# Hybrid decoder block on one core: second turns behind two columns, nine more small products, the first unit's tail in a hand-written order, and the second half's operands tied to the units

## The chip, the cores and the metric

One core of a Trainium2 chip runs the whole block in one launch. The metric is device time in microseconds (us), the median of several runs. TensorE (PE) multiplies, VectorE (DVE), ScalarE (ACT) and GpSimd (POOL) do the elementwise work, and SyncE (SP) issues all DMAs. Each engine works through its own queue in order.

## What is computed

The input is x, 2048 positions by 1024 features, in float32. The part that the change touches is the first third:

```
h    = rmsnorm(x, norm1_g)
proj = h @ w_in                      # 1024 x 3088
p_q, p_k, p_v, p_g, p_a, c_b, c_c, c_h = split(proj)
log_a  = log_sigmoid(p_a @ w_gate_up + b_gate) / 16
o_gla  = rmsnorm(gla_chunked(q, k, v, log_a)) * silu(p_g)
o_conv = c_b * conv3(c_c * c_h)
x = x + concat(o_gla, o_conv) @ w_out
x = x + (silu(h2 @ w_gate) * (h2 @ w_up)) @ w_down     # h2 = rmsnorm(x, norm2_g)
return rmsnorm(x, norm_f_g)
```

## The kernel before

**Number format.** Every large product is made of three passes: a float32 operand is split into a high part (`hi`, rounded on ACT) and a low part (`lo`, the difference, on DVE), and PE adds hi*hi, hi*lo and lo*hi (lines 412 to 414 and 686 to 688, each a 128x128 weight against 512 positions).

**Seven-product units.** Positions go in two halves of 1024, each of two blocks of 512. `unit` multiplies a 2x2 grid of weight quarters with a 2x2 grid of operand quarters in seven products instead of eight. The operands are B11, T1, T2, B21, T3, B22, T4, the weights A11, S1, S2, A12, S3, S4, A22, in that order. `unit_weights` loads the four raw quarters, makes S1 to S4 from them with four subtractions and additions (`mix`, line 384 or 386) and splits all seven (`weight_quarter`). One product is 12 matmuls. The products accumulate in PSUM; after products 4, 5 and 6 (indices 3, 4, 5) DVE adds a product to a kept tile (`plus`, line 443), and ACT copies others out (`copied`, line 450). Index 6 goes on in the bank that index 4 left (`oa`), so it must wait until `plus(c22, oa)` has read it.

**The opening.** For the first half the kernel begins with plain products, so that PE can start before the operands of the units exist. `opening` turns the rows of x with PE transposes (`turned(0)`: features 0 to 511, `turned(1)`: 512 to 1023, line 598), splits the turned tiles (`taken`), and adds up columns k = 0 to 7 for two rows of the weights (`column`). Twelve small products of a tile of ones precede it (`warm`, line 709). The squares for the norm (`square`, line 612) and the estimate of the norm's factor (`estimate`, `spread`) run on ACT and DVE beside it, and `turn` spreads the factor over the partitions with four PE transposes (line 652). Then come the columns of the second weight unit, the operands of the units (`normed`, `final`, `made`), the gate's small product (line 890), and the first unit, on `win[2]`.

**Order.** A planner places the instructions of each engine when the program is built, by their place in the program, by what is ready, and by its own estimates of durations. While the list `ordered` holds something, ACT's and DVE's instructions of the opening are chained by hand instead (`queued`), and a low part is issued only after the next high part (`late`, `catch_up`). `behind(marks)` puts instructions behind marked ones on the same engine, without a semaphore. The first unit's weights and its last operands, T3 and T4, are made in this chain; then `ordered` is cleared, and the unit's `plus` stand behind the chain's last low part (`given`).

**Background.** `tick` is called after every product and advances a list of generators by one step: at every tick while `hurry` holds, else at every second one. First come the gate's decays (`gate`, `forget_gate`) in turn with the squares of blocks 2 and 3 (`row_stats`), then `unhurried`, then `h1_ahead`, which makes the second half's operands: `combine` loads 16 tiles of x (`quad`), scales each on DVE (`scaled`, line 814), takes differences on POOL (lines 327 to 340), splits four of the seven kinds, and stores them. `gla_half` follows it. After the ten units of the first half (`in_proj(0)`: `win[2]`, then 3 to 11; 6 to 8 and 9 to 11 are the convolution's, with lines 966, 972 and 979 on DVE) the rest of `h1_ahead` is drained, and `load_pairs` loads the operands back.

## Time and profile before

| | |
|---|---|
| median of 3 runs | 2065.07 us (2064.35 to 2069.71) |
| the profiled execution, its own time | 2064.27 us |
| its span | 2062.5 us |
| mean granted TensorE clock over the span | 0.996 |
| busy, PE / DVE / ACT / POOL | 2024.1 / 1430.6 / 961.0 / 848.4 us |

The span runs from the first to the last recorded instruction; the run's own time is 1.8 us longer. In the views, L12 is line 12 of the kernel, "out<-in" names the tiles written and read, and the brackets at the end of a line of the timeline hold the idle time before that instruction and what ended it. A window's line gives the busy time of PE, PE's weight loads, DVE, ACT and POOL, then the granted clock as a share of full speed, the DMA engines' busy share and GB/s.

### The profile page before, as it was taken

The page shows a single profiled execution, that of the slowest core. Times are in us where ns is not written, and L with a number is a line of the kernel's source. Part 1 is how long each engine was busy: PE and PEld are TensorE (multiplying, and loading weights), DVE is VectorE, ACT ScalarE, POOL GpSimd, SP SyncE. Part 2 cuts the span into 40 slices and gives each one's busy share as a digit, 9 for nine tenths or more (in the row PEclk, how much of TensorE's full clock was granted, in tenths as well). Part 3 has the DMA queues.
Part 4 walks back from the last instruction along what each step waited for, and adds up shares of the span by engine and source line. Part 5 has one row for each costly group of instructions (what it writes and reads, how often), then busy time and mean ns, then how long its engine had stood idle before and what let it go on. Part 6 is the DMA issues. An engine that isn't in the chain of part 4 may idle for free.

```text
span 2062.5 us, 27137 instructions
## 1 busy us (share of the span) xinstructions
PE 2024.1 (98%) x9253; PEld 1660.3 (81%) x9253; DVE 1430.6 (69%) x2140; ACT 961.0 (47%) x1922; POOL 848.4 (41%) x618
## 2 busy tenths in 40 slices
PE   9999999999999999999999999999999999999997
PEld 7777888887888888888888888787888888888786
DVE  7888676559743786677676577776766666677774
ACT  5664455666543344444444452334434444453344
POOL 0136322222102474464464345533644554444544
PEclk9999999999999999999999999999999999999999
DMA  7378495425686873555444576476444444486653
GB/s 255 102 241 301 137 345 151 148 82 168 206 282 226 332 277 123 181 194 193 171 175 164 211 275 250 182 285 273 153 179 163 159 158 168 172 312 223 237 214 127
DMA packets 189738, 422.54 MB, mean 205 GB/s; under 512 B 19904, under 2 KB 65184, under 8 KB 180128
## 3 DMA queue, kind: packets, MB, share of 16 engines
q1 hardware_dynamic: 189600, 420.81, 57.6%
q8 instruction: 73, 1.20, 0.2%
q14 instruction: 65, 0.53, 0.1%
HBM read 276.02 MB, written 144.70 MB: 204 GB/s over the span
## 4 chain that ended last, share of the span: by engine, by line
PE 86%; DVE 7%; DMA 2%; ACT 2%; issue 1%; POOL 1%; SPq 0%; DVEq 0%; ACTq 0%; POOLq 0%
PE mm L412 24%; PE mm L414 24%; PE mm L413 24%; PE mm L1131 3%; PE mm L1132 3%; PE mm L1134 3%; DVE wq L192 2%; DMA op<-shT 1%; PE a_ps L890 1%; PE mm L688 1%; PE mm L686 1%; PE mm L687 1%; PE o_ps L1055 1%; PE o_ps L1057 1%; DVE op L192 1%
## 5 line engine op out<-in xcount | busy, mean ns | idle before, releaser
L412 PE MATMUL mm<-op,wq 128*128 128x512 f32 x2467 | 962.6, 393 | 14.9 <-ACT c L450 6.8
L413 PE MATMUL mm<-op,wq 128*128 128x512 f32 x2467 | 960.4, 390 | 0.3 <-DVE op L192 0.2
L414 PE MATMUL mm<-op,wq 128*128 128x512 f32 x2467 | 949.6, 390 | 4.3 <-DVE wq L192 4.2
L192 DVE TENSOR_TENSOR wq<-raw,wq 128x512 fp32r<-128x512 f32 (+2 forms) x612 | 495.3, 814 | 255.0 <-ACT wq L191 252.5
L191 ACT ACTIVATE wq<-raw 128x512 fp32r<-128x512 f32 (+2 forms) x612 | 355.6, 587 | 575.8 <-PE mm L414 441.3
L412 PEld LDWEIGHTS mm<-op,wq 128*128 128x128 f32 x2467 | 463.3, 188 | 120.0 <-ACT c L450 10.4
L414 PEld LDWEIGHTS mm<-op,wq 128*128 128x128 f32 x2467 | 463.3, 188 | 105.5 <-DVE wq L192 8.5
L413 PEld LDWEIGHTS mm<-op,wq 128*128 128x128 f32 x2467 | 463.7, 188 | 95.6 <-DVE op L192 1.8
L386 POOL TENSOR_TENSOR raw<-s,raw 128x512 f32<-128x512 f32 (+2 forms) x96 | 124.1, 1293 | 503.5 <-DVE wq L192 465.3
L386 POOL TENSOR_TENSOR raw<-raw 128x512 f32<-128x512 f32 (+2 forms) x192 | 255.0, 1334 | 123.6 <-DVE wq L192 118.9
L386 POOL TENSOR_TENSOR s<-raw 128x512 f32<-128x512 f32 (+2 forms) x96 | 126.4, 1317 | 290.5 <-DMA raw<-in_wffn_dram 83.6
L443 DVE TENSOR_TENSOR c<-mm,c 128x512 f32<-128x512 f32 x198 | 135.6, 686 | 69.0 <-PE mm L414 67.0
L443 DVE TENSOR_TENSOR y<-mm,y 128x512 f32<-128x512 f32 x185 | 126.9, 687 | 81.5 <-PE mm L414 80.9
L1113 POOL TENSOR_TENSOR ssx<-ssx,q 128x512 f32<-128x512 f32 x52 | 77.3, 1501 | 160.6 <-ACT q L1112 160.3
L450 ACT ACTIVATE c<-mm 128x512 f32<-128x512 f32 x198 | 115.6, 586 | 15.1 <-PE mm L414 12.9
L1131 PE MATMUL mm<-op,wq 128*128 128x512 f32 x256 | 100.9, 395 | 0.0
L1132 PE MATMUL mm<-op,wq 128*128 128x512 f32 x256 | 99.7, 390 | 0.0
L191 ACT ACTIVATE wq<-s 128x512 fp32r<-128x512 f32 (+2 forms) x96 | 56.1, 585 | 86.7 <-PE mm L414 83.8
L192 DVE TENSOR_TENSOR wq<-s,wq 128x512 fp32r<-128x512 f32 (+2 forms) x96 | 85.3, 888 | 2.8 <-ACT wq L191 2.1
L1134 PE MATMUL mm<-op,wq 128*128 128x512 f32 x256 | 79.7, 390 | 0.0
L192 DVE TENSOR_TENSOR op<-op 128x512 fp32r<-128x512 f32 x94 | 76.5, 841 | 4.3 <-ACT op L191 4.3
L1326 POOL TENSOR_TENSOR y<-x,y 128x512 f32<-128x512 f32 x32 | 53.7, 1678 | 44.7 <-DVE y L443 40.4
(222 smaller groups left out, 1845.9 us busy)
## 6 DMA issues: line engine op xcount, KB each, us to landing
raw<-in_wffn_dram SPq DMA_DIRECT2D x44, 1024.0 KB, 6.4
sa_B<-so SPq DMA_DIRECT2D x47, 512.0 KB, 4.3
op<-sa_B SPq DMA_DIRECT2D x47, 512.0 KB, 6.8
raw<-in_win_dram SPq DMA_DIRECT2D x22, 1024.0 KB, 5.9
sa_T<-so SPq DMA_DIRECT2D x44, 512.0 KB, 4.5
op<-sa_T SPq DMA_DIRECT2D x44, 512.0 KB, 6.6
raw<-in_wdown_dram SPq DMA_DIRECT2D x24, 768.0 KB, 5.5
sx<-y SPq DMA_DIRECT2D x48, 256.0 KB, 3.9
```

Of the source, the lines that this page charges most:

```text
L191: last_hi[:] = [act.activation(hi, src, AF.Copy)]
L192: last_lo[:] = [dve.tensor_tensor(lo, src, hi.bitcast(F32), ALU.subtract)]
L386: pool.tensor_tensor(*args)
L412: pe.matmul(o[:], wh, xh, start=first and k == 0, stop=False, skip_group_check=True)
L413: pe.matmul(o[:], wh, xl, start=False, stop=False, skip_group_check=True)
L414: return pe.matmul(o[:], wl, xh, start=False, stop=k == n - 1, skip_group_check=True)
L443: dve.tensor_tensor(t[:], o[:], t[:], ALU.add)
L450: last_out[:] = [act.activation(t[:], o[:], AF.Copy)]
L1113: pool.tensor_tensor(ssq[:], ssq[:], q[:], ALU.add)
L1131: pe.matmul(o[e, j][:], wh, m[:, 0, :], start=k == 0, stop=False)
L1132: pe.matmul(o[e, j][:], wh, m[:, 1, :], start=False, stop=False)
L1134: pe.matmul(o[e, j][:], wl, ops[k][j][:, 0, :], start=False, stop=k == KD - 1)
```

## The change

1. In `opening`, nine small products of ones follow `turned(0)`, and `turned(1)` is placed behind two columns (k = 0, 1) instead of three; column 2 moves behind it.
2. The first unit's tail stays in the hand-written chain. `T4` is no longer made before the unit's products but in a generator `rest`: tiles 0 and 1 ahead of `plus(c11, ...)`, tile 2 ahead of `plus(c22, ...)`, tile 3 behind it, then the split of A22; only then is `ordered` cleared, and `held` keeps the chain's last high and low part. The first two `plus` are links of the chain; the third stands behind `held`. The first five ticks return without a step of the background, and `row_stats` and the gate's copies stand behind `held`.
3. The second unit's mixing (`win[3]`) goes from POOL to DVE.
4. `h1_ahead` becomes `h1_paced`: each scaling stands behind the latest `plus` on DVE, and from `unhurried` on every fourth tick makes two steps until `h1_paced` ends.

```diff
 def tick():
     pace[0] += 1
+    if ordered:
+        return
     if pace[0] % 2 == 0 or hurry:
         step()
+        if steady and pace[0] % 4 == 0:
+            step()
...
 def unhurried():
     hurry.clear()
+    steady.append(True)
     yield
+
+def h1_paced():
+    with_marks.append(True)
+    yield from h1_ahead()
+    with_marks.clear()
+    steady.clear()
...
         def quad():
...
-            return scaled(col(g + k), rb[j], h)
+            with behind(last_plus if with_marks else []):
+                return scaled(col(g + k), rb[j], h)
...
         def mix(*args):
...
-                pool.tensor_tensor(*args)
+                eng.tensor_tensor(*args)
...
-        w["A22"] = weight_quarter(a22)
-        others()
+        w["A22"] = a22 if ordered else weight_quarter(a22)
...
-        given = []
-        if ordered:
-            catch_up()
-            ordered.clear()
-            given += last_lo
...
 def plus(t, o):
-    with behind(given):
-        dve.tensor_tensor(t[:], o[:], t[:], ALU.add)
+    if ordered:
+        queued(dve, lambda: dve.tensor_tensor(t[:], o[:], t[:], ALU.add))
+    else:
+        with behind(held if rest is not None else []):
+            last_plus[:] = [dve.tensor_tensor(t[:], o[:], t[:], ALU.add)]
     return t
...
-        plus(c11, mul(3))
+        o = mul(3)
+        then()
+        plus(c11, o)
         mul(4, oa)
+        then()
         plus(c22, oa)
+        if rest is not None:
+            next(rest, None)
+            w["A22"] = weight_quarter(w["A22"])
+            held[:] = last_hi + last_lo
+            ordered.clear()
         mul(5, ob)
...
-            with behind(last_out or unit_splits):
+            with behind(last_out + held):
...
         for j in range(2):
             stack = bx[0].tile([96, PB], F32R, name="a_sb", tag="b")
...
-            with behind(after):
+            with behind(held):
...
         turned(0)
+        for _ in range(9):
+            pe.matmul(warm[:, 0:P], ones[:], ones[:], start=True, stop=True)
...
-        for k in range(3):
+        for k in range(2):
             for r in range(2):
                 mark = column(0, 0, r, k)
         with behind([mark]):
             turned(1)
...
-        for k in range(3, 6):
+        for k in range(2, 6):
...
+        def rest():
+            difference("T4", 0)
+            difference("T4", 1)
+            yield
+            difference("T4", 2)
+            yield
+            difference("T4", 3)
+            h.clear()
...
-                yield unit(win[u], ops)
+                yield unit(win[u], ops, eng=dve if (half, u) == (0, 3) else pool)
```

More of the change, by code (lines that the diff above doesn't have):

```diff
@@ L801, in opening @@
         catch_up()
-        after = []
-        steps = gate(0, ops, mark, after)
+        steps = gate(0, ops, mark)
         next(steps)
@@ L806, in opening @@
         between = [
-            [lambda: out(1, 1, 0)], [lambda: out(1, 1, 1)], [partial(made, "T3"), lambda: after.extend(last_hi)], [],
-            [partial(made, "T4")],
-        ]
-        return ops, raw2, between, steps
+            [lambda: out(1, 1, 0)], [lambda: out(1, 1, 1)], [partial(made, "T3")],
+        ]
+        def rest():
[6 more added lines that the diff above has]
+            h.clear()
+        return ops, raw2, between, steps, rest()
     def scaled(g, rb, h, into=None):
@@ L876, in second_factor, with gate @@
         dve.memset(carry[:], 0.0)
-    def gate(half, ops, mark=None, after=()):
+    def gate(half, ops, mark=None):
         a = bank("a_ps")
@@ L939, in forget_gate, with in_proj @@
         store(s_d[b][i][:], t2[:])
-    def in_proj(half, ops, raw=None, between=()):
+    def in_proj(half, ops, raw=None, between=(), rest=None):
         def units():
             if half == 0:
-                yield unit(win[2], ops, raw=raw, between=between)
+                yield unit(win[2], ops, raw=raw, between=between, rest=rest)
             for u in range(0 if half else 3, 12):
-                yield unit(win[u], ops)
+                yield unit(win[u], ops, eng=dve if (half, u) == (0, 3) else pool)
         units = units()
@@ L1436, in tile_hymba_block @@
     act.preload_act_table_set("natural_log_exp_and_others")
-    ops, raw, between, steps = opening()
+    ops, raw, between, steps, rest = opening()
     hurry.append(True)
@@ L1440, in tile_hymba_block @@
         [
-            in_turn(steps, row_stats(2), row_stats(3)), unhurried(), h1_ahead(),
+            in_turn(steps, row_stats(2), row_stats(3)), unhurried(), h1_paced(),
         ]
     )
-    in_proj(0, ops, raw, between)
+    in_proj(0, ops, raw, between, rest)
     drain_background(lambda: len(background) < 2)
```

13 lines of the change are left out of this document (8 added, 5 removed).

## The prediction, made before the changed kernel was run

> **What bounds the kernel now.** I read the head of the page, then the chain that ended last, then PE's busy time by windows.
>
> ```profile
> span 2062.5 us, 27137 instructions
> PE 2024.1 (98%) x9253; PEld 1660.3 (81%) x9253; DVE 1430.6 (69%) x2140; ACT 961.0 (47%) x1922; POOL 848.4 (41%) x618
> ...
> PE 86%; DVE 7%; DMA 2%; ACT 2%; issue 1%; POOL 1%; SPq 0%; DVEq 0%; ACTq 0%; POOLq 0%
> ```
>
> PE is the bound: 86% of the last chain, and only 2062.5 - 2024.1 = 38.4 us of the span without a matmul. A change of order can win back idle time and time at a lower clock, nothing else. So the question is how much of both lies where the change reaches, the first 230 us.
>
> ```profile
> 60.00:92.00 32.00, 28.65 (x119) 23.01 (x118) 28.06 (x42) 18.63 (x39) 4.52 (x3) 0.95 0.24 73
> 92.00:132.00 40.00, 38.39 (x167) 30.41 (x166) 37.15 (x87) 30.54 (x71) 10.93 (x8) 1.00 0.69 230
> 132.00:176.00 44.00, 44.00 (x198) 36.44 (x197) 32.06 (x40) 22.06 (x38) 26.58 (x18) 1.00 0.83 283
> 176.00:216.00 40.00, 35.13 (x147) 26.65 (x146) 37.82 (x49) 19.32 (x41) 22.26 (x15) 1.00 0.77 247
> 216.00:256.00 40.00, 39.95 (x177) 32.76 (x176) 24.25 (x33) 15.24 (x31) 13.98 (x10) 1.00 0.35 124
> ```
>
> The second number of a row is PE's busy time. It falls short by 3.35 us in the stretch of the first unit, by 1.61 in the next, by nothing from 132 to 176, by 4.87 from 176 to 216, where DVE is busy 37.82 of 40 us, and by nothing again after that. The opening, before 60, is the fourth place.
>
> **Step 1, the opening.** PE's timeline, then ACT's and DVE's:
>
> ```profile
> 1.12 4.88 PE L709 MATMUL warm<-ones 128*128 128x128 f32 x24 [1.12 <-DVE ones L79]
> 5.84 2.49 PE L598 MATMUL xt<-ident,xr 128*128 128x128 f32 x16
> 10.33 0.51 PE L686 MATMUL mm<-op,wq 128*128 128x512 f32 x1 [2.00 <-ACT op L178]
> ...
> 16.73 1.91 PE L598 MATMUL xt<-ident,xr 128*128 128x128 f32 x16
> 18.40 0.48 PE L686 MATMUL mm<-op,wq 128*128 128x512 f32 x1
> ...
> 23.86 0.64 PE L652 MATMUL rb_ps<-ident,rep 128*128 128x128 f32 x4 [1.12 <-DVE rep L642]
> ```
> ```profile
> 15.15 0.19 ACT L612 ACTIVATION_READ_ACCUMULATOR q<-xr 128x1 f32 x1
> 18.35 0.69 ACT L178 ACTIVATE op<-xt,sml 128x512 fp32r<-128x512 f32 x1 [3.02 <-PE xt L598]
> ```
> ```profile
> 11.84 0.75 DVE L185 SCALAR_TENSOR_TENSOR op<-xt,sml,op 128x512 fp32r<-128x512 f32 x1
> 13.00 0.75 DVE L185 SCALAR_TENSOR_TENSOR op<-xt,sml,op 128x512 fp32r<-128x512 f32 x1 [0.41 <-ACT op L178]
> ```
> ```profile
> 13.00:14.00 1.00, 1.00 (x4) 0.71 (x4) 0.75 (x1) 1.00 (x3) 0.00 (x0) 0.50 1.09 422
> 16.00:17.00 1.00, 1.00 (x7) 0.78 (x6) 0.00 (x0) 0.00 (x0) 0.00 (x0) 1.00 1.04 406
> ```
>
> After the first turns (end 8.33) PE is idle for 2.00 us, and soon after that the granted clock is 0.50: 18 matmuls of three columns take 10.33 to 16.73. Behind them the second turns begin, and ACT, done with all else at 15.34, sits 3.02 us until they end. From there ACT and DVE lead the chain to the factor, for which PE waits 1.12 us at 23.86.
>
> The nine small products are 18 records (the twelve show as 24). I take 0.12 us each, as the turns of 16.73 have (1.91 / 16): 2.2 us, about the idle time; they end near 10.5, and the window in front of the columns is busy, so I take the clock as staying full. Two columns, 12 matmuls, then end with the low part of x's second tile (11.84 + 0.75 = 12.59) and two matmuls of 0.23 more: 13.1. The turns take 18.40 - 16.73 = 1.67 and end at 14.8, before ACT is free at 15.34. So ACT's chain moves by 18.35 - 15.34 = 3.0 us and no further, and the factor with it. Column 2, which now follows the turns, brings PE to 14.8 + 24 x 0.228 = 20.3, still ahead of the factor at 20.9. **Term: -3.0 us.** Bounds: if the clock falls as before, 12 matmuls last until 15.3, the turns until 17.0, and 1.4 us are won; if the small products run at the 0.203 us of the first twelve (4.88 / 24), they end at 12.0, 1.7 us late, and with a low clock behind them 0.3 us are lost. I take the upper end, because each cause is removed at its place; what is late next is ACT itself, whose order is unchanged.
>
> The Trainium skill, "TensorE: Matmul & The Clock Gate", Part 1, says that the gate watches windows of some 3.4 us which run free of the kernel's start. By that rule an idle time of 2 us lowers the clock in one execution and not in another. No second profile of this kernel is here to show it; what it would mean is the fourth rival.
>
> **Step 2, the first unit.** PE, its clock, and what DVE does meanwhile:
>
> ```profile
> 67.64 0.40 PE L412 MATMUL mm<-op,wq 128*128 128x512 f32 x1
> ...
> 83.83 0.39 PE L414 MATMUL mm<-op,wq 128*128 128x512 f32 x1
> 87.57 0.76 PE L412 MATMUL mm<-op,wq 128*128 128x512 f32 x1 [3.35 <-DVE c L443]
> ...
> 90.63 0.39 PE L413 MATMUL mm<-op,wq 128*128 128x512 f32 x1
> ```
> ```profile
> 88.00:89.00 1.00, 1.00 (x4) 0.71 (x4) 0.94 (x3) 0.00 (x0) 0.00 (x0) 0.50 0.63 205
> ```
> ```profile
> 64.01 0.69 DVE L384 TENSOR_TENSOR s<-raw 128x512 f32<-128x512 f32 x1
> ...
> 66.86 3.53 DVE L182 TENSOR_TENSOR wq<-raw,wq 128x512 fp32r<-128x512 f32 x2
> ...
> 75.74 1.29 DVE L182 TENSOR_TENSOR op<-h,op 128x512 fp32r<-128x512 f32 x2 [1.49 <-ACT op L178]
> ...
> 78.27 0.68 DVE L907 TENSOR_TENSOR a_sb<-a_ps,a_sb 32x512 fp32r<-32x512 f32 x1
> ...
> 85.42 0.69 DVE L182 TENSOR_TENSOR wq<-raw,wq 128x512 fp32r<-128x512 f32 x1
> 86.14 1.89 DVE L443 TENSOR_TENSOR c<-mm,c 128x512 f32<-128x512 f32 x3
> ```
> ```profile
> 66.84 1.30 POOL L386 TENSOR_TENSOR s<-raw 128x512 f32<-128x512 f32 x1 [65.03 <-DVE wq L182]
> ```
>
> Six products, 72 matmuls, run from 67.64 to 84.06: 0.228 us a matmul. The seventh waits until 87.57 for the second of three `plus`, which all stand behind the last low part of the chain, A22's at 85.42. That costs 3.51 us, and the restart at half clock (7 matmuls in 90.63 - 87.57 = 3.06 us instead of 1.60) costs 1.46 more: 4.97 together.
>
> DVE's work in front of that point holds three things that the change takes out. Two splits take 3.53 us where two others take 1.29 (75.74): 2.24 us beside POOL's first mixing at 66.84, which goes to DVE (three of 0.69, as at 64.01, later or in gaps). The gate's two differences, 1.36 us, go behind `held`. 1.49 us of waiting for ACT fall where ACT squares rows; these now come after the fifth tick. So A22's low part could end near 86.1 - 5.1 = 81.0, and with two `plus` (0.63 each) ahead of it, at 82.3.
>
> In the new order, c11's `plus` needs the end of product index 3 (78.6) and c22's that of index 4 (67.64 + 60 x 0.228 = 81.3). Behind the latter stand T4's last difference, two low parts and A22's, with `plus` five items of 0.60 to 0.63: 81.4 + 3.1 = 84.5. The seventh product's first two matmuls (from 84.06) need none of these low parts of A22, the third starts at 84.5. So a wait of 0 to 0.3 us is left, and no lower clock. **Term: -4.7 us.** Bounds: 0 if DVE still ends at 86, -5.0 if nothing waits.
>
> What is late next is the second unit. DVE then has, in a row, the third `plus` 0.6, A11's low part 0.6, three mixings 2.1, the gate's two differences 1.4 and S1's low part 0.6: 5.3 us from 84.5, so 89.8, where product index 1 needs S1's low part at 86.8 + 2.73 + 0.46 = 90.0. The gate's decays also move up against it, in the row 92:132 where DVE has only 2.85 us free. **Term: +1.0 us** (0 to +3). The delayed background costs PE nothing else: the five lost steps are made good by the doubled ones.
>
> **Step 3, the second half's operands.**
>
> ```profile
> 126.67 0.74 DVE L814 SCALAR_TENSOR_TENSOR h<-h,sml,rb_ps 128x512 f32<-128x512 f32 x1
> ...
> 192.35 0.74 DVE L814 SCALAR_TENSOR_TENSOR h<-h,sml,rb_ps 128x512 f32<-128x512 f32 x1
> 193.01 0.68 DVE L443 TENSOR_TENSOR c<-mm,c 128x512 f32<-128x512 f32 x1
> 193.61 1.77 DVE L192 TENSOR_TENSOR wq<-s,wq 128x512 fp32r<-128x512 f32 x1
> ```
> ```profile
> L814 DVE SCALAR_TENSOR_TENSOR h<-h,sml,rb_ps 128x512 f32<-128x512 f32 x6 | 4.4, 739 | 3.1 <-DMA h<-in_xt_dram 3.1
> ```
> ```profile
> 182.24 0.50 PE L412 MATMUL mm<-op,wq 128*128 128x512 f32 x1 [1.14 <-ACT c L450]
> ...
> 203.00 0.50 PE L414 MATMUL mm<-op,wq 128*128 128x512 f32 x1 [0.99 <-DVE wq L192]
> ```
>
> (The single row is the group of the scalings within 176 to 216: six.) The 16 scalings run from 126.67 to 192.35, a group of four in 16 us, though their ticks lie 38 us a group apart: the planner pulls them forward. Counted by ticks (2.73 us each), the changed ones begin at tick 28, near 143 on this trace's clock less what steps 1 and 2 save, and end at tick 60, near 231, a group in 25 us. In the convolution's first three units, where PE loses its 4.87 us, five scalings fall instead of six, evenly, and each behind a `plus` instead of ahead of it. I take a third of the loss: **-2.0 us**. Bounds: -5, all of it; upward, the third rival's price. The last scaling, at 231, lies 28 us ahead of the second half's start (67.64 + 70 x 2.73 = 259), and the row 216:256 has 15.75 us of DVE free for the group that slides there.
>
> **Sum:** -3.0 - 4.7 + 1.0 - 2.0 = -8.7 us. Against the profiled execution's own 2064.27 us that is 2055.6; the median of the runs shown lies 0.8 higher, so 2056.4 us. About 0.3%, 6.2 us, is what a measurement of this kernel can tell from no change.
>
> **The rivals.**
> - *Given back.* Steps 1 and 2 hold, but DVE stays full through the convolution (37.82 of 40 us with six scalings, and five plus their POOL differences are hardly fewer), so PE loses there what it lost, or the second unit loses 3 us. Against it: from 216 on DVE has room. Time: -6.7 to +0, 2058 to 2065, say 2061.
> - *All of it.* No stall is left up to 216: -3.0 - 5.0 - 1.6 - 4.9 = -14.5, 2050.6. Against it: a convolution's DVE load does not shrink.
> - *Slower.* The tie itself: a scaling behind a `plus` stands in front of the next weight's low part. It brings 0.74 us, its split 0.6, and a POOL difference that can hold DVE 1.1 us (193.61: 1.77 against 0.68), 2.4 us together. In 2.73 us of a product DVE owes PE a low part and 3/7 of a `plus`, 0.9 us, and about 0.6 to POOL's mixing: 1.2 us are free, 1.2 us over. If the four weight buffers do not absorb it, 16 x 1.2 = 19 us are lost in place of 4.9: -6.7 + 14 = +7.5, 2072.5. It decides once DVE is full between two `plus` throughout. For it: DVE at 95% from 176 to 216. Against it: DVE at 73% from 132 to 176 with nine scalings (16 less the first and these six), and no loss there.
> - *The clock would not have fallen.* If in the runs that make the median PE keeps its clock through the first 2.00 us, three columns end with the third tile's low part (13.75) near 14.3, the turns near 16.0, and only 16.0 - 15.3 = 0.7 us of the 3.0 are to be had: 2058.7. The Trainium skill's rule named above would give this. For the forecast: the one profile shows 0.50.
>
> **How the numbers follow.** Forecast (2051 to 2060) 0.45; given back 0.2; all of it, 0.1; slower 0.15; clock 0.1. Of the forecast all but 0.03 lies below 2058.9 (2065.07 - 6.2); of the clock's case and its spread half; of "given back" none. Faster: 0.42 + 0.1 + 0.04 = 0.56; same: 0.03 + 0.2 + 0.06 = 0.29; slower: 0.15. The range from 2050 to 2068 leaves out the slower case and a part of "all of it" below, 2 in 10.
>
> **What would show it.** Step 1: the second turns start near 13 instead of 16.73, the clock reads 1.00 from 12 to 16, the factor's transposes start near 20.9. Step 2: the seventh product follows the sixth without a gap, no row of half clock there, and the second unit starts some 7.5 us earlier than now (90.63 + 5 x 0.23 = 91.8). Step 3: scalings from about 135 to 222 and less than 4.87 us lost in the convolution's stretch. It is wrong if DVE's low parts end PE's idle time there more often than before, if the small products are placed where they delay the first column, or if new idle time appears past 260, where the operands are loaded back.

## The result and the profile after

| | before | after |
|---|---|---|
| median, runs of the comparison | 2067.29 us (11 runs) | 2072.09 us (11 runs) |
| ratio, 95% interval | | 1.0024 [1.0015, 1.0034] |
| the profiled execution, its own time | 2064.27 us | 2071.32 us |
| its span | 2062.5 us | 2069.5 us |

The changed kernel is slower by 0.24%. That is less than the 0.3% that the prediction took as the least that a measurement can tell from no change, but its interval lies wholly above 1, and 2072.09 us lies above the range of 2050 to 2068. The profiled spans differ by 7.0 us, in the same direction as the medians (4.8 us).

The head of the page, after:

```profile
span 2069.5 us, 27185 instructions
PE 2027.6 (98%) x9271; PEld 1662.7 (80%) x9271; DVE 1437.9 (69%) x2144; ACT 964.0 (47%) x1920; POOL 847.5 (41%) x614
```

PE has 18 instructions more (the nine small products), DVE four more and POOL four fewer (the second unit's mixing). ACT has two fewer, both loads of its function table (ACT_TABLE_LOAD, 13 in place of 15). The work is otherwise the same, so I look for the loss in the order. PE is without a matmul for 2069.5 - 2027.6 = 41.9 us in place of 38.4, and its busy time has grown by 3.5 us, which I put down to the small products and to matmuls at half clock.

Busy times by windows, after. All but the two past 256 are windows that the prediction shows for the kernel before; the second number is PE's busy time, the fourth DVE's, the seventh the granted clock:

```profile
60.00:92.00 32.00, 30.00 (x131) 24.07 (x130) 27.29 (x43) 19.97 (x39) 2.72 (x2) 1.00 0.32 109
92.00:132.00 40.00, 37.77 (x164) 29.75 (x163) 35.20 (x79) 28.77 (x69) 10.70 (x8) 1.00 0.63 214
...
280.00:300.00 20.00, 18.64 (x95) 15.19 (x95) 18.27 (x28) 13.63 (x34) 6.06 (x4) 1.00 1.00 362
300.00:320.00 20.00, 19.09 (x103) 14.40 (x103) 16.73 (x31) 12.79 (x34) 3.99 (x3) 1.00 0.84 264
```
```profile
176.00:216.00 40.00, 38.52 (x168) 30.82 (x167) 38.15 (x45) 16.35 (x33) 21.38 (x13) 1.00 0.50 167
216.00:256.00 40.00, 33.54 (x137) 26.26 (x136) 29.16 (x38) 16.91 (x34) 17.26 (x12) 0.91 0.73 237
```

The same windows past 256, before:

```profile
280.00:300.00 20.00, 20.00 (x104) 15.88 (x104) 16.21 (x30) 15.35 (x38) 4.88 (x5) 1.00 0.99 360
300.00:320.00 20.00, 20.00 (x112) 16.29 (x111) 16.17 (x27) 11.41 (x31) 5.09 (x4) 1.00 0.47 139
```

Read against the rows of before: PE gains in 60 to 92 (28.65 to 30.00 us) and in 176 to 216 (35.13 to 38.52). It then loses in 216 to 256 (39.95 to 33.54), in 280 to 300 (20.00 to 18.64) and in 300 to 320 (20.00 to 19.09). The stretch that was to take the second half's operands for nothing, 216 to 256, is where the gain was given back, and more.

In sums of the same view, PE's idle time falls by 2.86 us before 30 us and by 1.35 us from 60 to 92. It grows by 3.82 us from 92 to 256, gains and losses taken together, and by 3.75 us from 280 to 1000. So about half of the lost idle time lies in the second half's units and the attention, behind the stretch that the prediction's sum covers.

**What was won.** The opening's rows after, PE, then the clock:

```profile
13.45 1.91 PE L619 MATMUL xt<-ident,xr 128*128 128x128 f32 x16
...
20.69 0.60 PE L673 MATMUL rb_ps<-ident,rep 128*128 128x128 f32 x4
```
```profile
13.00:14.00 1.00, 1.00 (x9) 0.86 (x8) 0.57 (x2) 1.00 (x4) 0.00 (x0) 1.00 1.08 416
```

The second turns start at 13.45 in place of 16.73, the clock stays at 1.00, and the factor's transposes come at 20.69 in place of 23.86: 3.17 us, with no wait in front.

**What was left in the first unit.** PE, then ACT, then DVE:

```profile
82.88 0.50 PE L423 MATMUL mm<-op,wq 128*128 128x512 f32 x1 [1.93 <-ACT wq L178]
```
```profile
81.68 0.63 ACT L178 ACTIVATE op<-h 128x512 fp32r<-128x512 f32 x1 [1.17 <-DVE h L698]
82.22 0.61 ACT L178 ACTIVATE wq<-raw 128x512 fp32r<-128x512 f32 x1
```
```profile
80.36 0.68 DVE L449 TENSOR_TENSOR c<-mm,c 128x512 f32<-128x512 f32 x1
80.97 0.68 DVE L698 TENSOR_TENSOR h<-h 128x512 f32<-128x512 f32 x1
```

The seventh product starts at 82.88 in place of 87.57, 3.2 us of it from the opening, and no half clock follows in this profile. But 1.93 us of waiting are left. In the hand-written order the `plus` of c22 stands ahead of T4's last difference (80.97), ACT makes that tile's high part at 81.68, and A22's high part stands behind it on ACT, at 82.22. PE needs A22's high part for its very first matmul.

That the clock stays full here is luck. Of the kernels in this document fourteen have this new tail, and the profile of each has a wait of 1.92 or 1.93 us at this place. In five of them the clock stays at 1.00 (the changed kernel, e1, e9, e12, e14), in nine it falls to 0.50 behind the wait. So it does in e6, whose edit bears only on later instructions:

```profile
85.00:86.00 1.00, 1.00 (x3) 0.75 (x3) 0.84 (x2) 1.00 (x3) 0.00 (x0) 0.50 1.22 164
```

**Where it was lost.** PE around 221, then the clock there, then ACT, DVE and POOL in front of it:

```profile
221.32 0.80 PE L423 MATMUL mm<-op,wq 128*128 128x512 f32 x1 [4.37 <-ACT c L463]
...
250.78 0.50 PE L423 MATMUL mm<-op,wq 128*128 128x512 f32 x1 [2.02 <-ACT c L463]
```
```profile
222.00:224.00 2.00, 2.00 (x6) 1.57 (x5) 2.00 (x5) 0.80 (x2) 0.00 (x0) 0.50 0.99 362
```
```profile
218.60 0.63 ACT L191 ACTIVATE hi<-t 128x512 fp32r<-128x512 f32 x1 [5.25 <-POOL t L343]
219.13 1.14 ACT L191 ACTIVATE wq<-raw 128x512 fp32r<-128x512 f32 x2
...
220.69 1.06 ACT L463 ACTIVATE c<-mm 128x512 f32<-128x512 f32 x2
```
```profile
207.42 1.40 DVE L845 SCALAR_TENSOR_TENSOR h<-h,sml,rb_ps 128x512 f32<-128x512 f32 x2
...
211.45 1.78 DVE L192 TENSOR_TENSOR wq<-raw,wq 128x512 fp32r<-128x512 f32 x1
213.16 3.47 DVE L192 TENSOR_TENSOR c<-c,hi 128x512 fp32r<-128x512 f32 x2
216.55 0.68 DVE L192 TENSOR_TENSOR lo<-t,hi 128x512 fp32r<-128x512 f32 x1
...
237.64 0.73 DVE L845 SCALAR_TENSOR_TENSOR h<-h,sml,rb_ps 128x512 f32<-128x512 f32 x1
```
```profile
210.94 1.74 POOL L339 TENSOR_TENSOR t<-h 128x512 f32<-128x512 f32 x1
212.76 1.61 POOL L346 TENSOR_TENSOR h<-h 128x512 f32<-128x512 f32 x1
214.34 1.73 POOL L398 TENSOR_TENSOR raw<-raw 128x512 f32<-128x512 f32 x1
217.30 1.26 POOL L343 TENSOR_TENSOR t<-h,t 128x512 f32<-128x512 f32 x1 [1.23 <-DVE lo L192]
```

Read it from the bottom. Two scalings stand together at 207.42 (each behind a `plus`), so two POOL differences follow, at 210.94 and 212.76, with a mixing behind them. While these run, DVE's instructions beside them take 1.78 and 1.73 us in place of 0.68, so T1's low part comes only at 216.55. T2 (line 343) overwrites T1's tile, so POOL waits for that low part until 217.30; ACT has T2's high part (`hi<-t`) next in its order and waits 5.25 us for it. Behind it stand two weights' high parts (219.13), another high part and the copy of c11, for which PE waits 4.37 us, and the matmuls behind that run at half clock (six in 2.00 us at 222). The last scaling is at 237.64, where the kernel before had its last at 192.35.

### The profile page after: what moved, and what is told of

Its sections match the earlier page's. It is cut to its first block, busy times and chain, and to the rows that moved or that the text cites. A ratio compares the mean times of both kernels' runs of the same rounds, so it can differ in the third digit from the quotient of the medians.

```text
span 2069.5 us, 27185 instructions
## 1 busy us (share of the span) xinstructions
PE 2027.6 (98%) x9271; PEld 1662.7 (80%) x9271; DVE 1437.9 (69%) x2144; ACT 964.0 (47%) x1920; POOL 847.5 (41%) x614
## 4 chain that ended last, share of the span: by engine, by line
PE 85%; DVE 7%; ACT 2%; DMA 2%; issue 2%; POOL 1%; SPq 0%; DVEq 0%; ACTq 0%; POOLq 0%
PE mm L423 23%; PE mm L424 23%; PE mm L425 23%; PE mm L1162 3%; PE mm L1165 3%; PE mm L1163 3%; DVE wq L192 2%; DMA op<-shT 1%; PE mm L707 1%; PE a_ps L921 1%; PE mm L709 1%; PE mm L708 1%; PE o_ps L1086 1%; PE o_ps L1088 1%; DVE op L192 1%
## 5 line engine op out<-in xcount | busy, mean ns | idle before, releaser
L192 DVE TENSOR_TENSOR wq<-raw,wq 128x512 fp32r<-128x512 f32 (+2 forms) x612 | 502.3, 826 | 265.2 <-ACT wq L191 263.1
```

The source lines that it names most:

```text
L192: last_lo[:] = [dve.tensor_tensor(lo, src, hi.bitcast(F32), ALU.subtract)]
```

## The experiments

All ratios are against the kernel before, on the same chip, with 95% intervals. Parts are numbered as in the section on the change.

| run | what it is | median us | ratio |
|---|---|---|---|
| e7 | before + part 1 | 2064.60 | 0.9987 [0.9978, 0.9996] |
| e8 | the same without the nine small products | 2065.07 | 0.9993 [0.9984, 1.0003] |
| e1 | after without part 4 | 2067.60 | 1.0002 [0.9993, 1.0011] |
| e2 | before + part 4 | 2077.84 | 1.0051 [1.0038, 1.0064] |
| e3 | after, scalings not tied, doubled steps kept | 2072.93 | 1.0026 [1.0018, 1.0035] |
| e4 | after, tied, no doubled steps | 2092.23 | 1.0124 [1.0109, 1.0138] |
| e5 | after, attention five steps later | 2071.60 | 1.0026 [1.0016, 1.0035] |
| e6 | after, 16 differences on DVE | 2064.48 | 0.9992 [0.9983, 1.0000] |
| e9 | e1, 16 differences on DVE | 2064.91 | 0.9989 [0.9981, 0.9998] |
| e10 | before, 16 differences on DVE | 2063.44 | 0.9984 [0.9975, 0.9993] |
| e11 | e5 and e6 together | 2060.45 | 0.9966 [0.9953, 0.9978] |
| e12 | after, T1 and T2 split a step later | 2079.38 | 1.0056 [1.0044, 1.0069] |
| e13 | after, T1 and T2 on DVE | 2069.07 | 1.0001 [0.9991, 1.0010] |
| e14 | after, T3 and T4 on DVE | 2068.07 | 1.0003 [0.9994, 1.0012] |
| e15 | after, high parts of T1 and T2 on DVE | 2072.25 | 1.0026 [1.0016, 1.0037] |
| e16 | after, high parts of T1 and T2 on POOL | 2076.48 | 1.0042 [1.0029, 1.0055] |
| e17 | after, low parts of T1 and T2 replaced by a scaled copy made on ACT | 2068.56 | 1.0004 [0.9995, 1.0013] |
| e18 | e7 and e10 together | 2060.72 | 0.9972 [0.9963, 0.9982] |

### The parts, one by one

**e1, without part 4.** The marks and the doubled steps are never switched on, so the second half's operands come as they did:

```diff
 def unhurried():
     hurry.clear()
-    steady.append(True)
     yield
 def h1_paced():
-    with_marks.append(True)
     yield from h1_ahead()
```

> The changed kernel with part 4 undone: the scalings stand behind no plus, and no tick makes two steps. Theory T (the loss past 216 us comes from part 4: ACT and DVE meet the operands' instructions in the convolution): the stalls of 4.5, 2.2 and 1.5 us that the changed kernel shows at 221, 251 and 297 us go, while the opening (3.2 us won) and the first unit (2.7) stay; about 9 us faster than the kernel before, 2058, ratio 0.9955. Rival R (the background that starts five ticks later makes the operands late): the stalls past 216 stay in some form, ratio 1.000 to 1.003. Rival N (any change lets the planner scatter new stalls of this size): new ones elsewhere, ratio anywhere from 0.997 to 1.004.

Measured 1.0002: no gain at all, although the opening's and the first unit's gain is there. A part of it is given back where the operands now fall, by a wait of the same shape. ACT in e1, then PE (line 337 is T1's difference there):

```profile
159.47 0.63 ACT L191 ACTIVATE hi<-t 128x512 fp32r<-128x512 f32 x1 [5.02 <-POOL t L337]
```
```profile
161.65 0.50 PE L421 MATMUL mm<-op,wq 128*128 128x512 f32 x1 [2.98 <-ACT c L461]
```

So the simple theory, that the tie alone spends what the other parts win, falls: the untied operands spend a part of it too, some 60 us earlier. PE is idle for 4.06 us from 132 to 176, where the kernel before has no idle time. Another 3.4 us more than in the kernel before lie between 460 and 2000, in the slowest of e1's runs; what causes them stays open.

**e2, part 4 alone.**

```diff
 def unhurried():
     hurry.clear()
+    steady.append(True)
     yield
...
+            with behind(last_plus if with_marks else []):
+                return scaled(col(g + k), rb[j], h)
...
-                dve.tensor_tensor(t[:], o[:], t[:], ALU.add)
+                last_plus[:] = [dve.tensor_tensor(t[:], o[:], t[:], ALU.add)]
```

> The kernel before with part 4 alone: tie and doubled steps. Theory T: the first 130 us as in the kernel before, new stalls between 200 and 320 us of some 12 us, less what the tie saves ahead of the convolution (4 us): 5 to 12 us slower, ratio 1.0025 to 1.006. Rival R: no late background here, so no loss: ratio 0.998 to 1.000.

Measured 1.0051. PE's largest wait of its convolution stretch:

```profile
223.63 0.50 PE L422 MATMUL mm<-op,wq 128*128 128x512 f32 x1 [2.69 <-ACT c L460]
```

Part 4 costs time in either surrounding: 0.51% alone, and 1.0024 against 1.0002 in the whole. But e2's loss is for the most part not the one at 221. From 92 to 256 PE is idle for 7.25 us, and for 6.53 in the kernel before. Its largest wait comes later. PE, then ACT in front of it:

```profile
449.42 0.79 PE L422 MATMUL mm<-op,wq 128*128 128x512 f32 x1 [6.55 <-ACT wq L191]
```
```profile
446.96 1.28 ACT L492 ACT_TABLE_LOAD   x1
...
448.75 0.62 ACT L191 ACTIVATE wq<-raw 128x512 fp32r<-128x512 f32 x1
```

From 435 to 449 ACT loads its function table six times, 1.28 us each, as the gate's functions and the unit's alternate, and the high part that PE waits for stands behind them. Why they come together in e2 and not in the changed kernel, where PE is idle for 0.65 us from 320 to 460, is not shown.

**e3 and e4, the halves of part 4.** e3 leaves out `with_marks.append(True)`, e4 `steady.append(True)`.

> The changed kernel without the tie, its doubled steps kept. If the tie alone holds the scalings back into the convolution (theory T's first half), the stall of 4.5 us near 221 goes and the scalings end near 190; the stall at 251 (the gated attention's first loads ahead of ACT's copy) stays if the doubled steps cause it: ratio about 0.997. If the doubled steps are what matters, ratio about 1.002 as changed.

> The changed kernel with the tie but without doubled steps: a group of four scalings every 38 us instead of 25, the rest drained at the half's end. Theory T: the convolution's first three units see fewer of them, the stall near 221 shrinks, but the last groups are tied to the last plus of the half and come late, so that the second half's first units wait for operands: 5 us or more lost between 260 and 330; ratio 1.002 to 1.01. If only the density in the convolution counts, ratio 0.997.

e3 measured 1.0026, so without the tie, but with twice the steps, nothing is better than in the whole. Its waits lie earlier, as e1's do: PE is idle for 3.92 us from 132 to 176 and for 0.55 from 216 to 256, while 3.24 us stay from 460 to 480. e4 measured 1.0124: the operands come too late for the second half. PE's two largest waits there:

```profile
271.63 0.80 PE L422 MATMUL mm<-op,wq 128*128 128x512 f32 x1 [6.66 <-DVE c L451]
...
292.08 1.23 PE L1061 MATMUL sc<-kq 64*128 64x128 f32 x8 [15.83 <-DVE kq L1051]
```

The first ends with a `plus`. The second is for the attention's keys: SP issues their loads from 285.25 on, behind the last store of the operands at 284.61, and the exponential that goes into them waits 11.19 us on ACT for its load. The doubled steps are needed by the tie, and they are the part of the change that also moves the attention behind `h1_paced` forward.

**e7 and e8, part 1 alone, with and without the nine small products.** The edit of e8 is the moved column without the two lines of the loop:

```diff
-        for k in range(3):
+        for k in range(2):
...
-        for k in range(3, 6):
+        for k in range(2, 6):
```

> The kernel before with part 1 alone. By step 1 of the prediction the second turns start near 13.4, the factor's transposes near 20.6 instead of 23.86, and everything up to 60 us is 3.2 us early; 3 us in the median, ratio 0.9985, if nothing later gives it back. Rival (the clock's windows run free, so the kernel before does not always lose them): 0.5 to 1.5 us, ratio 0.9993 to 1.000. Rival N (the planner places the later operands anew and the gain is lost in the convolution): ratio 1.000 to 1.003 with the first 60 us still early.

> Part 1 without the nine small products: the turns behind two columns only. If the idle time of 2 us lowers the clock, 12 matmuls at half clock end near 15.3 and the turns start there: about 1.4 us won of 3.2 in the first 60 us; without a fall of the clock the turns start near 13.5 and all is won without them.

Part 1 alone gives 0.9987, 2.7 us of 2066.54 (0.8 to 4.5 by the interval), near its term of 3.0. Without the small products 0.9993 is measured; the two intervals overlap, so the timing does not separate them. The two profiles differ: in e8 the clock falls to 0.50 from 13 to 14 and the factor's transposes come at 22.51, in e7 it stays at 1.00 and they come at 21.31, against 23.86 in the kernel before. Parts 2 and 3 then seem to take back what part 1 gives: 0.9987 with part 1, 1.0002 with parts 1 to 3, with intervals that overlap from 0.9993 to 0.9996.

### What the loss at 221 hangs on

**e12, the splits a step later.** The split of T1 and T2 is moved behind the next `yield` and behind ACT's latest copy:

```diff
-            put("T2", k, t1)
             yield
+            with behind(last_out if with_marks else []):
+                put("T2", k, t1)
```

and so for T1.

> The changed kernel, differences on POOL as they were, but the splits of T1 and T2 one step later and on ACT behind the latest copy. It tells two parts of theory U apart. If it is the high part's place at the head of ACT's queue that costs, the waits of ACT for POOL (5.25 and 3.4 us) and the stall at 221 go though POOL still holds DVE: ratio 0.999 to 1.001. If POOL's hold on DVE is what costs, the stall stays, on another wait: ratio 1.002 or more.

At the same place ACT still waits 5.25 us for POOL's difference (at 218.70), so the edit did not do what it was made for, and its 1.0056 separates no theories. Much of its further loss lies from 280 to 320, where PE is idle for 7.95 us.

**e6, e9 and e10, the sixteen differences on DVE,** in the whole, in e1, and in the kernel before:

```diff
-    def combine(src, g, rb, put):
+    def combine(src, g, rb, put, eng=pool):
...
-            pool.tensor_tensor(t1[:], b12[:], b11[:], ALU.subtract)
+            eng.tensor_tensor(t1[:], b12[:], b11[:], ALU.subtract)
```

and so for the other three; the call in `h1_ahead` passes `dve`.

> The changed kernel with the 16 differences of the second half's operands on DVE instead of POOL. Theory U (what PE waits for is ACT's copy, and ACT's queue is held by the high part of a difference that POOL has not finished): POOL's 1.7 us and its place in POOL's queue are gone, ACT's waits of 5.25 and 3.4 us for the difference (218.6, 238.9) vanish, and with them the stall at 221 and its half clock, 6.7 us. The stall of 2.2 us at 251, behind the gated attention's loads, stays, and the later ones. About 2065, ratio 0.999. Rival V (it is DVE's load in the convolution: 16 differences of 0.6 us more on DVE make it worse): ratio 1.003 or more, with PE waiting for DVE.

> The kernel without tie and doubled steps (which came to 1.0002), again with the 16 differences on DVE. Theory U: its ACT waits of 5.0 and 5.5 us at 159 and 179 for POOL's difference vanish, with the PE stalls of 4.4 us at 156 to 162 and some of the 3 us at 197 to 204; what the opening and the first unit won then stays: 7 to 10 us under the kernel before, ratio 0.9955 to 0.997. Rival V: DVE busier, PE waits for DVE instead, ratio 1.000 or more.

> The kernel before with only the 16 differences on DVE. Theory U: ACT's waits for POOL at 158, 172, 180 and 187 vanish, of PE's 6 us between 180 and 216 the first 1.3 to 2 go: ratio 0.998 to 1.000. Rival V: ratio 1.001 or more.

0.9992, 0.9989, 0.9984: this edit wins 0.32% in the whole, 0.16% in the kernel before, and 0.13% in e1, where the two intervals overlap. It gives sixteen instructions more to the engine that is full. DVE's total in e6 is 1433.4 us, 4.5 less than in the changed kernel, but that is not shown to be the edit's doing: e7 and e8 have equally many DVE instructions and totals of 1424.5 and 1436.6, and e9's total is 0.2 us above e1's. From 92 to 256 us DVE is busy for 143.00 us in e6 against 136.06 in the changed kernel, and POOL for 48.19 against 71.38, while PE gets more done.

PE and ACT in e6 where the loss was:

```profile
217.31 0.50 PE L423 MATMUL mm<-op,wq 128*128 128x512 f32 x1 [2.50 <-ACT c L463]
```
```profile
215.11 0.63 ACT L191 ACTIVATE hi<-t 128x512 fp32r<-128x512 f32 x1 [2.58 <-DVE t L343]
```

The wait is 2.50 us in place of 4.37, it ends 4 us earlier, and no half clock follows here. But the edit does two things: ACT no longer waits for POOL, and POOL no longer lengthens DVE's instructions. Two theories were left: Q, that ACT's order is at fault (a high part at its head, the copies behind it), and H, that DVE is full and held by POOL, which makes that high part's operand late.

**e13 and e14, one half of the differences each.** Only T1 and T2 are split, so only these can stand at ACT's head. e13 has lines 339 and 343 on DVE, e14 lines 346 and 352.

> The changed kernel with only the differences T1 and T2 of the convolution's input on DVE, eight of the sixteen; T3 and T4 stay on POOL. T1 and T2 are split on ACT and DVE for the next products, T3 and T4 are stored whole. Theory Q (ACT's in-order queue: a high part at its head waits for POOL's difference, and the copies behind it wait with it): only T1 and T2 can make ACT wait for POOL, so this removes all of it: the idle of 4.37 us at 221 us and most of the twelve matmuls at half clock go, and the ratio to before is that of all sixteen on DVE, 0.9985 to 0.9997. Rival theory H (what costs is that POOL, while it runs, makes DVE's own instructions longer, 0.68 us to 1.77): half of the sixteen holds are left, so half of the gain: 1.0005 to 1.0015, and a stall of 2 us or more is left near 221.

> The other half alone: the changed kernel with only T3 and T4 on DVE, T1 and T2 left on POOL. Theory Q: ACT's high part of T2 still waits for POOL, so a stall of 3 us or more stays in the stretch from 205 to 230 us, and the time is that of the changed kernel, ratio 1.0015 to 1.003. Theory H: half of the holds go, half of the gain comes, 1.0005 to 1.0015, the same as with T1 and T2. If this one is as fast as all sixteen (0.999) and the one with T1 and T2 is not, both are wrong and it is T3's and T4's place in POOL's queue, ahead of the mixes, that delays T2.

Measured 1.0001 and 1.0003, the same within their intervals. Both intervals overlap with H's range of 1.0005 to 1.0015. Q's range for e13, 0.9985 to 0.9997, overlaps as well, but its range for e14, 1.0015 to 1.003, lies above the interval measured. ACT in e13, then in e14:

```profile
216.56 0.63 ACT L191 ACTIVATE hi<-t 128x512 fp32r<-128x512 f32 x1 [4.25 <-DVE t L343]
```
```profile
218.63 0.63 ACT L191 ACTIVATE hi<-t 128x512 fp32r<-128x512 f32 x1 [3.69 <-POOL t L343]
```

In both the high part is still late, in e13 by DVE alone, and PE still waits 3.39 and 3.62 us. This speaks for H. That each half gained more than half of e6's gain is within the noise.

**e15 and e16, the high parts of T1 and T2 taken off ACT,** on DVE or on POOL:

```diff
-            split(h[:], hi[:], lo[:])
+            if n in ("T1", "T2") and not ordered:
+                last_hi[:] = [dve.tensor_copy(hi[:], h[:])]
+                top = hi[:].bitcast(F32)
+                last_lo[:] = [dve.tensor_tensor(lo[:], h[:], top, ALU.subtract)]
+            else:
+                split(h[:], hi[:], lo[:])
```

> The changed kernel with all sixteen differences on POOL as they are, but the high parts of T1 and T2 (eight copies of 128 x 512) made on DVE in place of ACT. ACT then never has an operand at its head that POOL has still to make; DVE gets eight instructions more. Theory Q (the copies wait behind the high part at the head of ACT's queue): ACT's idle of 5.25 us at 218.60 and PE's of 4.37 at 221 go, ratio 0.999 to 1.0005, though DVE has more to do. Rival theory H (it is DVE that is full, and the chain of T2 is late for that): DVE is fuller, its low parts and pluses come later, and the time is that of the changed kernel or worse, 1.0024 to 1.004, with PE's idle now ended by DVE's plus or by a low part.

> The same eight high parts on POOL, which is busy for about half of the stretch from 132 to 216 us. ACT again never waits for POOL's difference. Theory Q: PE's idle of 4.37 us at 221 goes, ratio 0.999 to 1.001. Theory H: POOL runs longer beside DVE and holds it more, and T2's low part on DVE waits for one POOL instruction more: 1.003 to 1.006.

Measured 1.0026 and 1.0042: nothing won by the first, 0.18% lost by the second. PE and ACT in e15:

```profile
221.19 0.80 PE L423 MATMUL mm<-op,wq 128*128 128x512 f32 x1 [4.20 <-ACT c L463]
```
```profile
220.02 0.63 ACT L191 ACTIVATE hi<-c 128x512 fp32r<-128x512 f32 x1 [2.78 <-DVE c L1015]
```

PE's wait is 4.20 us with no T2 on ACT at all. The copy of c11 now stands behind another high part that waits for DVE. So Q falls as far as it names T2's high part. The copy still stands behind a late high part in ACT's order, and e15 does not take that link away. In e16 Q's wait does shrink: PE waits 2.71 us at 218.93 and no more near 251, and ACT waits 2.67 us for POOL's mixing instead. The time is lost from 280 to 320, where PE is idle for 6.83 us against 2.27 in the changed kernel; why is not shown. So e16's ratio does not speak against Q.

**e17, the reverse: ACT keeps the high parts, DVE is lighter by eight low parts.** In place of the low parts ACT writes a scaled copy of the source, eight instructions more for ACT, so these operands lack their true low part.

```diff
+            if n in ("T1", "T2") and not ordered:
+                last_hi[:] = [act.activation(hi[:], h[:], AF.Copy)]
+                last_lo[:] = [act.activation(lo[:], h[:], AF.Copy, scale=2.0**-12)]
```

> The changed kernel, differences on POOL, high parts on ACT as they were, but the low parts of T1 and T2 are taken off DVE: ACT writes the high part's source times 2 to the power -12 in their place (eight instructions), so these operands lack their true low part. Theory Q (a high part at the head of ACT's queue that waits for POOL): that wait is still there and ACT has eight instructions more, so 1.002 to 1.004, with PE's idle near 221 as before. Theory H (DVE is full from 176 to 216 us, and held by POOL, so the chain of differences is late): DVE loses eight instructions of 0.68 to 1.78 us, T2 no longer waits for a low part on DVE, and the ratio falls to 0.999 to 1.001, with PE's idle near 221 under 2 us.

Measured 1.0004, inside what H expected and below what Q expected. H's other number failed: PE still waits 4.72 us at 220.20, since ACT still waits for POOL, whose difference now stands behind the mixing on POOL itself. ACT, then POOL, in e17:

```profile
216.44 0.63 ACT L871 ACTIVATE hi<-t 128x512 fp32r<-128x512 f32 x1 [3.91 <-POOL t L343]
```
```profile
213.00 1.74 POOL L398 TENSOR_TENSOR raw<-raw 128x512 f32<-128x512 f32 x1
214.69 1.71 POOL L343 TENSOR_TENSOR t<-h,t 128x512 f32<-128x512 f32 x1
```

PE starts again 1.1 us earlier than in the changed kernel (220.20 against 221.32), and the wait at 251 is gone: PE is busy all of 230 to 256.

```profile
230.00:256.00 26.00, 26.00 (x120) 20.78 (x119) 20.51 (x30) 13.64 (x29) 11.95 (x8) 1.00 0.67 204
```

Taken together: the edits that take differences off POOL (e6, e13, e14) and the one that takes low parts off DVE (e17) win 0.2 to 0.3%; eight high parts more on DVE (e15) or on POOL (e16) win nothing. That fits a stretch in which DVE and POOL together are short of time and ACT is not. It does not fit DVE's load alone, because e6, e13 and e14 give DVE more to do. What is not settled is the share of each link. The chain DVE, POOL, ACT goes through three in-order engines, and no run removed one link and left the other two untouched.

### The losses behind 240, and a version that gains

**e5, the attention later.** Five empty steps stand at the end of `h1_paced`, because the doubled steps bring the attention's first steps forward into the end of the convolution:

```diff
         steady.clear()
+        for _ in range(5):
+            yield
```

> The changed kernel with five empty steps behind the second half's operands, so that the gated attention's first loads have a later place than the first half's last products. If the early place of the attention is what holds ACT at 249 (an exponential that waits 5.4 us for its load, ahead of the copy that PE waits for), the 2.2 us at 251 go and perhaps the collision of loads near 297 to 305 (3 us): ratio 1.000 to 1.0015 instead of 1.0024. If the planner pulls the loads forward regardless of their place, nothing changes.

ACT and PE in the changed kernel, for what this was to remove:

```profile
249.38 0.42 ACT L1049 ACTIVATE ee<-ee 128x256 f32<-128x256 f32 x1 [5.40 <-DMA ee<-sd]
```
```profile
467.67 0.72 PE L1062 MATMUL sc<-kq 64*128 64x128 f32 x8 [3.23 <-DVE kq L1052]
```

The last of these in the kernel before:

```profile
481.93 0.71 PE L1031 MATMUL sc<-kq 64*128 64x128 f32 x8 [1.28 <-DVE kq L1021]
```

The exponential of the attention stands in ACT's order with its operand still in a DMA, and the copy for PE's 250.78 stands behind it. In e5's profile the window 300 to 320 is full again:

```profile
300.00:320.00 20.00, 20.00 (x100) 15.17 (x99) 13.81 (x28) 11.96 (x33) 4.25 (x3) 1.00 0.75 210
```

the wait for the keys is back at 1.28 us (at 485.06), and the span is 2067.8 us. But the wait at 251 stays (1.99 us), the profiled run is 1.8 us faster than e5's median, and the median does not show the gain: 1.0026. By itself the edit is not shown to help.

**e11, e5 and e6 together.**

> The changed kernel with both repairs: differences on DVE, and five empty steps ahead of the gated attention. If the two losses are separate (the ACT queue held by POOL's difference near 221, 6.7 us with its half clock; the attention's early place, 6 us of stalls between 290 and 470 in the changed kernel that are gone with the empty steps), they add: some 38.7 - 4 - 3 - 5 = 26 to 27 us of stalls over the run instead of 38.7, 5 us under the kernel before: ratio 0.9965 to 0.998. If they are one loss that only moves, ratio 0.999 to 1.001.

0.9966 [0.9953, 0.9978], the lowest ratio of all, by the medians 6.1 us under the 2066.54 us of the kernel before. Against e6's 0.9992 the five steps now help; the intervals do not overlap.

**e18, part 1 and the differences alone,** without parts 2 to 4.

> The kernel before with part 1 of the change alone (the second turns behind two columns, nine small products) and the sixteen differences on DVE; parts 2, 3 and 4 left out. Alone, part 1 gave 0.9987 and the differences 0.9984. If the two add up, because the differences' move frees DVE in the stretch where the opening's gain was lost, 0.997 (0.9960 to 0.9980), and parts 2 to 4 then bring nothing beyond it: the changed kernel with both repairs had 0.9966. If the opening's gain is lost again in the convolution's stretch, 0.9980 to 0.9990, and parts 2 to 4 are needed for the rest.

0.9972 [0.9963, 0.9982]: the two gains add up (0.9987 x 0.9984 = 0.9971), and e11's interval overlaps with it. Parts 2 to 4 are not shown to bring anything beyond.

## Why the prediction was wrong

- **Step 1, -3.0 us: right.** 3.17 us in the trace, 2.7 us by e7's ratio. The turns were at 13.45 (said: near 13), the clock at 1.00, the transposes at 20.69 (said: 20.9).
- **Step 2, -4.7 us: the mechanism was right in part, the size was off.** The unit restarts earlier, but 1.93 us of waiting are left where "a wait of 0 to 0.3 us" was said. In this profile 3.35 + 1.46 - 1.93 = 2.9 us are won. The 1.46 us of them that come from the clock are luck: where it falls behind the wait, as in nine of the fourteen profiles with this tail, about 3.35 - 1.93 = 1.4 us are won. The working followed DVE alone and looked for A22's low part; the first matmul needs A22's high part, which the hand-written order puts on ACT behind T4's last high part, and so behind the `plus` of c22.
- **What is late next, +1.0 us: the size came near, by chance.** PE's idle time in 92 to 132 grew from 1.61 to 2.23 us. But nothing waits for S1's low part, as the working had it; the waits are at 107.53, 121.57 and 125.76, and among the profiles with the same tail the idle time of this window goes from 1.48 (e5) to 2.29 us (e14).
- **Step 3, -2.0 us: the step that failed.** Less is lost from 176 to 216, as said: PE idles 1.48 us in place of 4.87, 3.4 us less. It is not for the reason given, because six scalings fall there (from 177.18 to 207.42) and not five, in bunches, and DVE is as full as before (38.15 us). What failed is "the row 216:256 has 15.75 us of DVE free for the group that slides there". The row now has 10.84 us free (40 - 29.16), so there was room in the sum; but PE idles 6.46 us there in place of 0.05. The operands do not come evenly, they come in bunches behind a `plus` (three at 144.00, two at 207.42), each with a POOL difference, two conversions and a low part that wait for each other across DVE, POOL and ACT, and in the same ACT queue stand the copies that PE waits for. Free time in a window's mean is no cover for such a chain. The last scaling came at 237.64 and not at 231. The half clock behind the wait adds to the loss.
- **A second step failed, a term put at nothing.** The prediction says "The delayed background costs PE nothing else: the five lost steps are made good by the doubled ones." New idle time past 260, which it names as a sign of being wrong, came: 2.27 us in the windows 280 to 320, and 3.23 us of waiting at 467.67 in place of 1.28. The doubled steps were counted as moving the operands only; they move everything behind them in the background as well, the attention first. The profiles of e5 and e11 bear this out (1.28 us again, at 485.06 and 474.55); e5's median does not by itself.
- **The rival "slower"** had 2072.5 us, and 2072.09 came. Its condition, a full DVE, holds from 176 to 216 (38.15 of 40 us), but there PE lost less than before, and it does not hold in the window where the loss came (29.16 of 40). Its mechanism is not what happened: it had a small loss at each of 16 scalings, ended by a weight's low part on DVE, and the trace has one large wait at 221 and a few behind it, ended by ACT's copies. That its number fits is chance.
- **The rival "given back"** is nearest to the mechanism, with the place wrong: the loss came past 216, where it was thought impossible. e1 shows that it happens without part 4 as well, at 160.
- **The rival "clock"** is in part borne out. e2 has the opening of the kernel before, and kept its clock after a wait of 2.16 us; e10 has it too, and did not, after 2.13 us. e2's row, then e10's:

```profile
12.00:13.00 1.00, 1.00 (x6) 0.76 (x6) 1.00 (x2) 1.00 (x4) 0.00 (x0) 1.00 1.05 404
```
```profile
12.00:13.00 1.00, 1.00 (x4) 0.81 (x3) 0.69 (x2) 1.00 (x4) 0.00 (x0) 0.50 1.04 401
```

So where the clock holds, a part of the opening's gain is not to be had: e2's factor comes to PE at 22.58, which leaves 1.9 of the 3.17 us. The Trainium skill, "TensorE: Matmul & The Clock Gate", Part 1, says that the clock's windows run free of the kernel's start; these two rows agree with it. That an idle time of 2 us then lowers the clock in one execution and not in another is the prediction's own inference; these rows and the fourteen profiles above bear it out. By e7's ratio 2.7 us were won all the same.

## What to carry to other kernels

Where a chain of small steps crosses several in-order engines, cost it as a chain with its place in each engine's order, and ask what stands behind its waiting head; the free time of a window's mean does not hide it. Before an operation is moved off a full engine, look at how long the full engine's instructions become while the other one runs: here sixteen differences moved back onto the fullest engine won 0.32% in one kernel and 0.16% in another. A step counter that is sped up moves everything behind it, so look at what comes next in that list. A clock that falls in one profile need not fall in the next, so look at several profiles before a term of a sum is put on it.

## What the runs showed of the hardware

- Beside a POOL difference of 128 x 512, DVE's own instruction of that size took 1.78 us (211.45 in the changed kernel); with POOL idle it took 0.68 (216.55).
- PE's clock fell to 0.50 after waits of 2.00 us (the opening of the kernel before), 2.13 us (the opening of e10), 3.35 us (the kernel before, at 87.57) and 4.37 us. It stayed at 1.00 after waits of 2.16 us (e2's opening), 2.50 us (e6, at 217.31), 2.98 us (e1, at 161.65) and 3.35 us (e2, at 86.28). After the wait of 1.92 or 1.93 us in the new tail it fell in nine profiles of fourteen. So the length of the wait alone does not decide it.
- A load of ACT's function table took 1.28 us. Six of them between 435 and 449 us in e2 stood in front of a high part for which PE waited 6.55 us.
